# A recurrence's value side: one pair of heads at a time, or two pairs side by side

## The chip, the cores and the metric

The kernel runs on one core of a Trainium2 chip. The metric is the device time of one execution in microseconds. The engines are TensorE (PE, with its weight loads listed as PEld), VectorE (DVE), ScalarE (ACT), GpSimd (POOL) and SyncE (SP), whose queue issues the transfers.

## The reference, cut to what matters

Two decoder layers on 256 tokens of width 2048, in fp32. The first is an RWKV-7 layer with an MLP, the second an attention layer with an MLP. The change lies in the RWKV layer. Its core is a scan over time with a 64x64 state for each of 32 heads, behind it a normalisation over each head, a bonus term, a gate and an output product:

```python
def step(S, inp):
    r_t, w_t, k_t, v_t, a_t, b_t = inp
    sa = jnp.einsum('bhvk,bhk->bhv', S, a_t)
    S = S * w_t[:, :, None, :] + sa[..., None] * b_t[:, :, None, :] + v_t[..., None] * k_t[:, :, None, :]
    y_t = jnp.einsum('bhvk,bhk->bhv', S, r_t)
    return S, y_t
...
y = (y - mu) * lax.rsqrt(var + GN_EPS)
y = y * ln_w.astype(f32).reshape(h, n) + ln_b.astype(f32).reshape(h, n)
y = y + jnp.sum(rh * kh * r_k.astype(f32), axis=-1, keepdims=True) * vh
return (y * g) @ w_out
```

## The kernel before, in words

**Products.** All large products are made of two-part numbers: a weight is split into a high part `wh` (ACT, line 146) and a low part `wl` (DVE, line 147), 512 columns at a time, in `high_low`. Each part comes from a pool of three buffers. `product` makes 128 columns of r or v: sixteen steps, each one wide matmul of 512 columns (line 348) and one of 256 with the low part (line 350); four steps use one split, and each step is reckoned at 0.32.

**The scan.** Time is cut into four chunks of 64 (`NCH`). Heads go in pairs: head 0 on partitions 0 to 63, head 1 on 64 to 127. The key side (`key_low` to `merges`) has made for each pair a triangular inverse `XT` and scaled copies of its inputs and put them to memory (`sp`). The value side then runs the 16 pairs one after the other. `prep_load` brings a pair's data back (`S1b`), `prep` makes the scores `SC` (`sc`, line 908) and the transposes (`bt`, lines 926 to 928), `bonus` the bonus term, and `chain` goes through the chunks: `g` from the scores and the state `SV` (line 966), R times the state into `y` (972), `sa` = `XT` times `G` (976), `sp` the new part of the state (983), the scores times `ST` into `y` (996). DVE carries each result to the next step; POOL makes `Se`, the decayed old state (994), which DVE adds (990). `post` normalises on DVE and POOL; `post_pe` makes the gate with `g2` (line 689), transposes the result (1034), and ACT, POOL and DVE make z from it (1036 to 1041), the input of the output product `wout`.

**What sets the order.** On PE the order is that of the program text (`rwkv_in_order`). Between two dependent steps `chain` calls `hop`, 11 times a pair. A hop first takes what hangs at its number in `extra` (PR: the two parts of the next pair's `prep` at hops 5 and 8; the bonus at 2; `post_pe` of the last pair, loads and splits at hop 2, matmuls at hop 6), subtracts what it is reckoned at from `target`, and `fill`s the rest with steps of the products for later pairs, or at the end of `wout` (`out_part`, lines 681 to 683). The other engines run in an order that the scheduler sets by priority in program order. PSUM has eight banks: two each of `acc`, `ps` and `mg`, one each of `y` and `gn`; `g`, `sa` and `sp` take `mg` in turn, `y` the bank of its name, `post_pe` takes `gn`. The pool `xb` has 16 tiles, at this point for z; `xa` has 32, for the two parts of r's and v's inputs.

Of the kernel before, what the change touches and what calls it, by code (L numbers as in the profile page):

```python
# [17 lines left out]
P = 128  # L18
T = 256
# [76 lines left out]
S1W = 7 * T + 4  # L96


def s1_views(x):
    def c3(a, w=64):  # L100
        return x[:, a:a + NCH * w].rearrange("p (c t) -> p c t", c=NCH)
    bk = x[:, 2 * T:4 * T].rearrange("p (c a t) -> p c a t", c=NCH, a=2)
    return c3(0), c3(T), bk, x[:, 4 * T:5 * T], c3(5 * T, 65), c3(6 * T + 4)


class K:
# [125 lines left out]
    def rstd_row(self, rs, name):  # L232
        nc = self.nc
        ps = self.ps(f"rb_{name}")
        for t in range(2):
            dg = self.sm.tile([P, P], F32, tag="dg", name=f"dg_{name}{t}")
            nc.vector.tensor_scalar(dg, self.c("ident"), rs[:, t:t + 1], None, ALU.mult)
            nc.tensor.matmul(ps[:, t * P:(t + 1) * P], self.ones, dg, start=True, stop=True)
# [29 lines left out]
    def run(self):  # L268
        tc, nc, d = self.tc, self.nc, self.d
        with ExitStack() as es:  # L270
# [6 lines left out]
            self.ones = self.cp.tile([P, P], F32, name="ones")  # L277
# [3 lines left out]
            nc.vector.memset(self.ones, 1.0)  # L281
# [74 lines left out]
    def rwkv(self):  # L356
        tc, nc, d = self.tc, self.nc, self.d
        with ExitStack() as es:
# [3 lines left out]
            self.queue, self.due, self.ob = deque(), 0.0, {}  # L362
            self.side, self.sdue = deque(), 0.0


            self.sp = [dr.tile([2, P, S1W - T], F32, name=f"sp{c}") for c in range(NPAIR // 2)]
            self.za = [dr.tile([64, 32, 64], F32, name=f"za{i}") for i in range(2)]
# [100 lines left out]
            self.hwa = [wk.tile([96, 2, T], F32R, name=f"hwa{i}") for i in range(2)]  # L468
# [55 lines left out]
            merge = chain.from_iterable(self.merges(c, ats) for c in range(8))  # L524
# [46 lines left out]
            ready = set()  # L571

            def products():
                while stream:
                    p, i = stream.popleft()
                    yield from rv_product(p, i)
                    if i == 2:
                        ready.add(p)

# [23 lines left out]
            for p in range(NPAIR):  # L603
                if p in (1, 2):
                    merge_steps(4)
                if p == 13:
                    self.queue.append(take(w0, 28))
                extra = deque([(2, self.bonus(p, rvs[p], st[p]))])
                if p > 0:
                    pe = self.post_pe(p - 1, post, zs)  # L610
                    extra += [(PH - PG, pe), (PH, pe)]
                if p + 1 < NPAIR:
                    st[p + 1] = self.prep_load(p + 1)
                    need(p + 1)
                    pr = self.prep(p + 1, rvs[p + 1], st[p + 1])
# [3 lines left out]
                if p == NPAIR - 1:  # L619
                    extra.insert(1, (2, start(w1)))  # L620
                hop = [0]
                target = (left / (NPAIR - p) + LP) / 11
# [9 lines left out]
                yps = self.chain(p, st.pop(p), hopf)  # L632
                while extra:
                    next(extra.popleft()[1], None)
                post = self.post(p, yps, self.ob[p])
            self.fill(100.0)
            self.drain(self.post_pe(NPAIR - 1, post, zs))
# [127 lines left out]
    def key_mid(self, p, k, side):  # L765
# [12 lines left out]
        for j in J:  # L778
            _, A, BK, kp, E, _ = V[j]
# [4 lines left out]
            nc.sync.dma_start(self.sp[p // 2][j, :, :S1W - 2 * T], S1[j][:, T:S1W - T])  # L784
# [3 lines left out]
    def key_high(self, p, V, ats):  # L788
        nc, wk = self.nc, self.wk
        H = [slice(0, 64), slice(64, 128)]  # L790
        for j in range(2):
            q = p + j
            _, A, BK, _, _, _ = V[j]
# [4 lines left out]
            AT = wk.tile([P, NCH, 64], F32, tag="t1", bufs=10, name=f"AT{q}")  # L798
# [32 lines left out]
    def merges(self, c, ats):  # L831
# [17 lines left out]
        off = two("mk", "mk")[1]  # L849
# [17 lines left out]
        Q, Qv = two("sv", "Q")  # L867
# [9 lines left out]
        Qv = two("sv", "Q32")[1]  # L877
# [6 lines left out]
        nc.sync.dma_start(self.sp[c][:, :, S1W - 2 * T:].rearrange("i p t -> p i t"),  # L884
# [3 lines left out]
    def prep_load(self, p):  # L888
        S1 = self.wk.tile([P, S1W], F32, tag="S1", bufs=2, name=f"S1b_{p}")
        self.nc.sync.dma_start(S1[:, T:], self.sp[p // 2][p % 2])  # L890
        return {"S1": S1}


    def prep(self, p, rv, st):
        nc, wk = self.nc, self.wk
        S1 = st["S1"]
        R, A, BK, kp, E, XT = s1_views(S1)
        RA = S1[:, :2 * T].rearrange("p (a c t) -> p c a t", a=2, c=NCH)
        H = [slice(0, 64), slice(64, 128)]
        r, v = rv[:, :T], rv[:, T:]  # L900
        nc.vector.tensor_tensor(R, self.c4(r), E[:, :, 1:], ALU.mult)

        SC = [[None] * NCH for _ in range(2)]
        msc = self.c("msc")
        pss = [self.ps(f"sc{p}{h}").rearrange("p (c t) -> p c t", c=NCH) for h in range(2)]
        for c in range(NCH):
            for h in range(2):
                nc.tensor.matmul(pss[h][:, c, :], BK[H[h], c].rearrange("p a t -> p (a t)"), RA[H[h], c],
                                 start=True, stop=True)
        for a in (0, 2):  # L910
            for h in range(2):
                x = wk.tile([P, 2, P], F32, tag="t1", bufs=10, name=f"SC{p}{h}{a}")
                nc.vector.tensor_tensor(x, pss[h][:, a:a + 2], msc.unsqueeze(1).broadcast_to([P, 2, P]), ALU.mult)
                nc.gpsimd.tensor_copy(x[H[h], :, 64:], A[H[h], a:a + 2])
                SC[h][a], SC[h][a + 1] = x[:, 0], x[:, 1]
        yield 1.75

        kr = [H[1], H[0]]
        idh = [self.c("ident")[x, x] for x in H]
        ST = self.t2("st", f"ST{p}").rearrange("p (c h t) -> p c h t", c=NCH, h=2)  # L920
        SV = self.t2("sv", f"SV{p}").rearrange("p (c h t) -> p c h t", c=NCH, h=2)
        BT = self.t2("bt", f"BT{p}").rearrange("p (h c t) -> p h c t", c=NCH, h=2)
        pss = [self.ps(f"bt{p}{h}").rearrange("p (c t) -> p c t", t=64) for h in range(2)]
        for c in range(NCH):
            for h in range(2):
                nc.tensor.transpose(pss[h][:, c, :], BK[H[h], c].rearrange("p a t -> p (a t)"), idh[h])
            nc.tensor.transpose(pss[0][:, 4 + c, :], rv[H[0], T - 64 + 64 * c:T + 64 + 64 * c], idh[0])
            nc.tensor.transpose(pss[1][:64, 4 + c, :], v[H[1], 64 * c:64 * c + 64], idh[1])
        for h in range(2):
            nc.scalar.activation(ST[kr[h], :, h, :], pss[h][kr[h], 4:8, :], AF.Copy)  # L930
            nc.scalar.activation(BT[:, h], pss[h][:, :4, :], AF.Copy)
            nc.gpsimd.tensor_copy(SV[kr[h], :, h, :], ST[kr[h], :, h, :])
        st.update(R=R, E=E, XT=XT, SC=SC, ST=ST, SV=SV, BT=BT)
        yield 0.9

    def bonus(self, p, rv, st):
        nc = self.nc
        r, v = rv[:, :T], rv[:, T:]
        ob = self.t2("ei", f"ob{p}")
        self.ob[p] = ob  # L940
        bv = ob[:, T:]
        nc.vector.scalar_tensor_tensor(bv, r, self.vec("r_k", p), s1_views(st["S1"])[3], ALU.mult, ALU.mult)
        bps = self.ps(f"bon{p}")
        bh = self.wk.tile([P, 2, T], F32R, tag="nr", bufs=WB["nr"], name=f"bh{p}")
        nc.gpsimd.tensor_copy(bh[:, 0], bv)
        nc.vector.tensor_tensor(bh[:, 1], bv, bh[:, 0].bitcast(F32), ALU.subtract)
        for i in range(2):
            nc.tensor.matmul(bps[:, :T], self.bones, bh[:, i], start=(i == 0), stop=(i == 1))
        nc.vector.tensor_tensor(bv, bps[:, :T], v, ALU.mult)
        yield 0.43  # L950


    def chain(self, p, st, hop):
# [3 lines left out]
        R, E, XT, SC, ST, SV, BT = (st[n] for n in ("R", "E", "XT", "SC", "ST", "SV", "BT"))  # L957
        yps = self.ps(f"y{p}", "y")
        for c in range(NCH):
            first = c == 0  # L960
            g = self.ps(f"g{p}{c}", "mg")
            for h in range(2):
                if first:
                    nc.tensor.matmul(g[H[h], :64], SC[h][c][kr[h], 64:], SV[kr[h], c, h, :], start=True, stop=True)
                else:
                    nc.tensor.matmul(g[H[h], :64], SC[h][c][:, 64:], SV[:, c, h, :], start=True, stop=True)
            G = wk.tile([P, 64], F32, tag="G", bufs=2, name=f"G{p}{c}")
            nc.vector.tensor_copy(G, g[:, :64])
            ys = [yps[H[h], c * 64:(c + 1) * 64] for h in range(2)]
            if not first:  # L970
# [312 lines left out]
```

## Time and profile before

| | us |
|---|---|
| median of 3 runs | 2420.58 (2420.09 to 2421.37) |
| the profiled execution | 2418.55 |
| its span | 2416.4 |
| PE busy | 2337.0 (97%) |
| DVE busy | 1558.5 (64%) |
| ACT busy | 1283.8 (53%) |
| POOL busy | 483.0 (20%) |

The span runs from the first to the last instruction of the program; 2.15 us of the execution lie around it. Busy time is the union of an engine's instructions. Matmuls are pipelined and their ends are modelled, so PE's cost is better read from one instruction's start to the next one's start. The key side takes the first 300 us, the value side about 310 to 683 us; the rest is MLP, attention and MLP.

### The profile page before, as it was taken

Reading aid. Unit: us, or ns where it says so; the run is one execution under the profiler, and the core shown is the slowest. Engines: PE = TensorE matmul, PEld = TensorE weight load, DVE = VectorE, ACT = ScalarE, POOL = GpSimd, SP = SyncE. Lnnn points to the kernel's source line nnn. Section 1 sums busy time; section 2 is a strip of 40 time slices with the busy share of each in tenths; the row PEclk is TensorE's granted clock in tenths of the full one; section 3 lists DMA queues with packets and bytes.
Section 4 is the critical chain, followed back from the end, with each engine's and each line's share of the span. In section 5 each row is a group of like instructions: output and inputs, shape, how many; then the busy total and the mean of one; then the engine's idle time right before and its main releaser. Section 6 shows DMA issues by size and latency. Waiting matters only on the chain. (4 is left out here: it accounts for less than half of the span.)

```text
span 2416.4 us, 40472 instructions
## 1 busy us (share of the span) xinstructions
PE 2337.0 (97%) x14448; PEld 1925.1 (80%) x14448; DVE 1558.5 (64%) x3126; ACT 1283.8 (53%) x2563; POOL 483.0 (20%) x635
## 2 busy tenths in 40 slices
PE   5887899999999999999999999999999999999999
PEld 4676677777788888888888887777888888888887
DVE  7887667777666556556556666765655655655655
ACT  5545333333356546546546565665654554654654
POOL 3657322333201101001001001641110110110100
PEclk9999899999999999999999999999999999999999
DMA  4666544444465555555555555334555555555565
GB/s 140 203 197 180 165 144 147 142 142 140 147 198 183 191 189 192 187 195 188 192 192 188 189 185 178 114 114 153 187 187 195 189 189 193 191 189 195 186 199 174
DMA packets 149642, 425.64 MB, mean 176 GB/s; under 512 B 38848, under 2 KB 46784, under 8 KB 149440
## 3 DMA queue, kind: packets, MB, share of 16 engines
q1 hardware_dynamic: 148000, 420.62, 53.1%
q8 instruction: 113, 1.85, 0.3%
q10 hardware_dynamic: 1440, 2.44, 0.3%
q14 instruction: 89, 0.73, 0.1%
HBM read 403.05 MB, written 19.96 MB: 175 GB/s over the span
## 5 line engine op out<-in xcount | busy, mean ns | idle before, releaser
L169 PE MATMUL ps_u<-x_m,wh_u 128*128 128x512 f32 x2048 | 559.1, 394 | 0.0
L147 DVE TENSOR_TENSOR wl_d<-raw_d,wh_d 128x512 fp32r<-128x512 f32 x512 | 355.7, 695 | 293.6 <-ACT wh_d L146 274.4
L147 DVE TENSOR_TENSOR wl_u<-raw_u,wh_u 128x512 fp32r<-128x512 f32 x512 | 354.5, 693 | 263.4 <-ACT wh_u L146 253.7
L146 ACT ACTIVATE wh_d<-raw_d 128x512 fp32r<-128x512 f32 x512 | 323.6, 632 | 351.9 <-DVE wl_d L147 261.3
L146 ACT ACTIVATE wh_u<-raw_u 128x512 fp32r<-128x512 f32 x512 | 323.7, 633 | 246.2 <-PE ps_u L169 227.7
L187 PE MATMUL ps_d<-wl_d,h 128*128 128x512 f32 x1024 | 399.0, 390 | 1.2 <-DVE wl_d L147 1.2
L185 PE MATMUL ps_d<-wh_d,h 128*128 128x512 f32 x1024 | 398.7, 389 | 0.0
L186 PE MATMUL ps_d<-wh_d,h 128*128 128x512 f32 x1024 | 398.6, 389 | 0.0
L169 PEld LDWEIGHTS ps_u<-x_m,wh_u 128*128 128x128 f32 x2048 | 350.6, 189 | 47.6 <-ACT wh_u L146 0.2
L173 PEld LDWEIGHTS ps_u<-x_m,wl_u 128*128 128x128 f32 x2048 | 313.8, 189 | 43.1
L1065 POOL TENSOR_TENSOR h<-w,h 128x256 fp32r<-128x256 f32 x128 | 114.0, 892 | 1117.6 <-ACT h L1064 1079.1
L173 PE MATMUL ps_u<-x_m,wl_u 128*128 128x256 f32 x2048 | 325.7, 281 | 0.0
L187 PEld LDWEIGHTS ps_d<-wl_d,h 128*128 128x128 f32 x1024 | 192.2, 188 | 41.5 <-DVE wl_d L147 1.6
L185 PEld LDWEIGHTS ps_d<-wh_d,h 128*128 128x128 f32 x1024 | 192.2, 188 | 39.8
L186 PEld LDWEIGHTS ps_d<-wh_d,h 128*128 128x128 f32 x1024 | 192.2, 188 | 39.4
L348 PE MATMUL ps_k<-lk,wh_k 128*128 128x512 f32 x256 | 98.1, 420 | 7.0 <-DVE lk L417 6.3
L348 PE MATMUL ps_v<-lv,wh_v 128*128 128x512 f32 x256 | 103.5, 432 | 0.0
L348 PE MATMUL ps_r<-lr,wh_r 128*128 128x512 f32 x256 | 102.9, 431 | 0.0
L146 ACT ACTIVATE wh_v<-raw_v 128x512 fp32r<-128x512 f32 x64 | 40.4, 631 | 94.7 <-PE ps_r L348 36.2
L146 ACT ACTIVATE wh_r<-raw_r 128x512 fp32r<-128x512 f32 x64 | 40.3, 630 | 79.8 <-PE ps_v L348 32.9
L350 PE MATMUL ps_k<-lk,wl_k 128*128 128x256 f32 x256 | 74.9, 292 | 6.3 <-DVE wl_k L147 6.3
L1222 POOL TENSOR_SCALAR s<-s,den 128x128 f32<-128x128 f32 x64 | 61.8, 981 | 77.3 <-DVE den L1218 30.5
(308 smaller groups left out, 3747.3 us busy)
## 6 DMA issues: line engine op xcount, KB each, us to landing
raw_u<-in_up SPq DMA_DIRECT2D x256, 512.0 KB
raw_d<-in_down SPq DMA_DIRECT2D x256, 512.0 KB
raw_k<-in_wrkv SPq DMA_DIRECT2D x32, 512.0 KB
raw_r<-in_wrkv SPq DMA_DIRECT2D x32, 512.0 KB
raw_v<-in_wrkv SPq DMA_DIRECT2D x32, 512.0 KB
raw_wout<-in_wout SPq DMA_DIRECT2D x32, 512.0 KB
raw_q<-in_wq SPq DMA_DIRECT2D x32, 512.0 KB
S1b<-sp SPq DMA_DIRECT2D x16, 770.0 KB
```

The source lines that it names most:

```text
L146: nc.scalar.activation(wh, src, AF.Copy)
L147: nc.vector.tensor_tensor(wl, src, wh.bitcast(F32), ALU.subtract)
L169: nc.tensor.matmul(ps, wh[:, j * P:(j + 1) * P], xt[kt].rearrange("p a t -> p (a t)"), start=(kt == 0), stop=False, skip_group_check=True)
L173: nc.tensor.matmul(ps[:, :T], wl[:, j * P:(j + 1) * P], xt[kt][:, 0, :], start=False, stop=(kt == KT - 1), skip_group_check=True)
L185: nc.tensor.matmul(pss[t], xt[kb][:, 0, tt], wh, start=(kb == 0), stop=False)
L186: nc.tensor.matmul(pss[t], xt[kb][:, 1, tt], wh, start=False, stop=False)
L187: nc.tensor.matmul(pss[t], xt[kb][:, 0, tt], wl, start=False, stop=(kb == nk - 1))
L348: nc.tensor.matmul(ps, wh[:, j * P:(j + 1) * P], xt[kt].rearrange("p a t -> p (a t)"), start=(kt == 0), stop=False, skip_group_check=True)
L350: nc.tensor.matmul(ps[:, :T], wl[:, j * P:(j + 1) * P], xt[kt][:, 0, :], start=False, stop=(kt == KT - 1), skip_group_check=True)
L1065: nc.gpsimd.tensor_tensor(hx[:, 1, :], w, hx[:, 0, :].bitcast(F32), ALU.subtract)
L1222: nc.gpsimd.tensor_scalar(ss[i][:, sl[t]], ss[i][:, sl[t]], den[:, i, t:t + 1], None, ALU.mult)
```

## The change

Two pairs (a duo) go through `chain` together, so that the loop runs 8 times. Each step is issued for both pairs, into one bank; the carrying copies of the second pair go to ACT instead of DVE. R times the state stands behind `sa` instead of behind `g`. The decayed old state is no longer made on POOL and added on DVE: PE adds the old state to `sp` with a matmul by the identity (chunks 1 and 2), and the decay is applied once when the sum is carried out. Four of the second pair's tiles (RX, ST, SV, BT) come from `xb`; `XT` is put to memory by itself (`sx`) and loaded beside a copy of R, so `S1b` is shorter. `prep` makes the bonus too and hangs in six parts at hops 5 to 10, and asks for its pair's products (`need`) there. `post_pe` takes two g2 tiles at hop 2, makes both pairs at hop 4 and takes both banks of `mg`; its result waits in `zf` until all products are made (`self.made`), and `split_z` makes z from it, for the first half in `xa`. The merges of 6 and 7 move from between the first pairs into hops 1 to 4 of duo 0. `wout` is queued at hop 10 of duo 6 and hop 2 of duo 7. `rstd_row` makes its matrix of ones when it is called. Lines that leave stand in the functions above; of `post` only the loop over two pairs is new.

```diff
...
-PH, PR = 6, (5, 8)
-PG = 4
+PG, PH, PR = 2, 4, (5, 6, 7, 8, 9, 10)
 PB = dict(acc=2, ps=2, mg=2, y=1, gn=1)
-WB = dict(rv=3, bt=2, st=2, sv=2, ta=2, sq=2, ei=2, nr=2, mk=1)
+WB = dict(rv=3, bt=2, st=2, sv=2, ta=2, sq=2, ei=2, nr=2, mk=1, rx=2, hb=2)
...
+            ND = NPAIR // 2
+            for u in range(ND):
+                extra = deque()
+                if u == 0:
+                    late = [self.merges(c, ats) for c in (6, 7)]
+                    extra += [(k, m) for k in (1, 2, 3, 4) for m in late]
+                if u > 0:
+                    pe = self.post_pe(u - 1, post, zs)
+                    extra += [(PG, pe), (PH, pe)]
+                if u + 1 < ND:
+                    st[u + 1] = self.prep_load(u + 1)
+                    pr = self.prep(u + 1, rvs, st[u + 1], need)
                     extra += [(k, pr) for k in PR]
+                if u == ND - 2:
+                    extra.append((PR[-1], start(w0)))
+                if u == ND - 1:
+                    extra.append((2, start(w1)))
                 left = len(stream) * 5.1 + LW
                 extra = deque(sorted(extra, key=lambda e: e[0]))
                 hop = [0]
+                target = (left / (ND - u) + LP) / 11
                 def hopf():
...
+    def duo(self, tag, j, name):
+        return self.xlt(name, F32, "xb") if j else self.t2(tag, name)
+    def prep_load(self, u):
+        res = []
+        for j in range(2):
+            S1 = self.wk.tile([P, S1W], F32, tag="S1", bufs=2, name=f"S1b_{2 * u + j}")
+            self.nc.sync.dma_start(S1[:, T:], self.sp[u][j])
+            RX = self.duo("rx", j, f"RX{2 * u + j}")
+            self.nc.sync.dma_start(RX[:, T:], self.sx[u][j])
+            res.append({"S1": S1, "RX": RX})
...
+    def prep(self, u, rvs, sts, need=None):
...
+        for j in range(2):
+            p, st = 2 * u + j, sts[j]
+            if need:
+                need(p)
...
+            nc.vector.tensor_tensor(R, self.c4(r), E[:, :, 1:], ALU.mult)
+            st["R"], st["XT"] = self.c4(st["RX"][:, :T]), self.c4(st["RX"][:, T:])
+            nc.gpsimd.tensor_copy(st["R"], R)
+            st["eC"] = self.sm.tile([P, NCH], F32, tag="eC", bufs=4, name=f"eC{p}")
+            nc.gpsimd.tensor_copy(st["eC"], E[:, :, 64])
+            st["bv"] = bv
...
+            yield 1.3
...
+            ST = self.duo("st", j, f"ST{p}").rearrange("p (c h t) -> p c h t", c=NCH, h=2)
+            SV = self.duo("sv", j, f"SV{p}").rearrange("p (c h t) -> p c h t", c=NCH, h=2)
+            BT = self.duo("bt", j, f"BT{p}").rearrange("p (h c t) -> p h c t", c=NCH, h=2)
...
+            st.update(ST=ST, SV=SV, BT=BT)
...
+            yield 0.8
...
+            yield 0.25
...
+    def chain(self, u, sts, hop):
...
+        yps = [self.ps(f"y{2 * u + j}", ("y", "gn")[j]) for j in J]
+        def bank(nm, c):
+            return self.ps(f"{nm}{u}{c}", "mg")[:, :P].rearrange("p (j t) -> p j t", j=2)
         for c in range(NCH):
+            first, last = c == 0, c == NCH - 1
+            g = bank("g", c)
+            for j in J:
+                for h in range(2):
+                    x = kr[h] if first else full
+                    nc.tensor.matmul(g[H[h], j], SC[j][h][c][x, 64:], SV[j][x, c, h, :], start=True, stop=True)
+            G = wk.tile([P, 2, 64], F32, tag="G", bufs=2, name=f"G{u}{c}")
+            nc.vector.tensor_copy(G, g)
+            hop()
+            sap = bank("sa", c)
+            for j in J:
+                for h in range(2):
+                    nc.tensor.matmul(sap[H[h], j], XT[j][H[h], c, :], G[H[h], j], start=True, stop=True)
             for h in range(2):
+                nc.vector.tensor_copy(ST[0][H[h], c, h, :], sap[H[h], 0])
+                nc.scalar.activation(ST[1][H[h], c, h, :], sap[H[h], 1], AF.Copy)
+            ys = [[yps[j][H[h], c * 64:(c + 1) * 64] for h in range(2)] for j in J]
             if not first:
+                for j in J:
+                    for h in range(2):
+                        nc.tensor.matmul(ys[j][h], R[j][H[h], c, :], SV[j][H[h], c, h, :], start=True, stop=False)
+            hop()
+            if not last:
+                sp = bank("sp", c)
+                for j in J:
+                    if not first:
+                        for h in range(2):
+                            nc.tensor.matmul(sp[H[h], j], ident[:, H[h]], SV[j][:, c, h, :], start=True, stop=False)
+                    for h in range(2):
+                        nc.tensor.matmul(sp[H[h], j], BT[j][:, h, c, :], ST[j][:, c, h, :], start=first, stop=True)
                 for h in range(2):
+                    nc.vector.tensor_scalar(SV[0][H[h], c + 1, h, :], sp[H[h], 0], eC[0][H[h], c:c + 1], None, ALU.mult)
+                    nc.scalar.activation(SV[1][H[h], c + 1, h, :], sp[H[h], 1], AF.Copy, scale=eC[1][H[h], c:c + 1])
+            for j in J:
                 for h in range(2):
+                    nc.tensor.matmul(ys[j][h], SC[j][h][c][:, :64], ST[j][:, c, h, :], start=first, stop=True)
+            if not last:
                 hop()
         return yps
...
+    def post_pe(self, u, post, zs):
+        nc = self.nc
+        lg = []
+        for j in range(2):
+            raw = self.load(self.d["g2"][2 * u + j].rearrange("p a c -> p (a c)"), f"g2_{2 * u + j}")[0][:, :2 * P]
+            lg.append(self.high_low(raw, f"g2_{2 * u + j}"))
         yield 0.0
         H = [slice(0, 64), slice(64, 128)]
+        zf = self.xlt(f"zf{u}", F32, "xb").rearrange("p (j t) -> p j t", j=2)
+        pss = [self.ps(f"yt{2 * u + j}", "mg") for j in range(2)]
         for j in range(2):
+            for i in range(2):
+                self.three(pss[j][:, T:], [x[:, i * P:i * P + P] for x in lg[j]], [x[:, i] for x in self.sg], i == 0, i == 1)
+        for j in range(2):
+            p, (yc, bv) = 2 * u + j, post[j]
+            yt, gp = pss[j][:, :T], pss[j][:, T:]
+            for c in range(NCH):
+                for h in range(2):
+                    nc.tensor.matmul(yt[H[h], c * 64:(c + 1) * 64], yc[H[h], c, :], self.c("ident")[H[h], H[h]],
+                                     start=True, stop=True)
+            o = self.t2("ei", f"o{p}")[:, :T]
+            nc.scalar.activation(o, yt, AF.Identity, bias=self.vec("ln_b", p), scale=self.vec("ln_w", p))
+            nc.gpsimd.tensor_tensor(o, o, bv, ALU.add)
+            nc.vector.tensor_tensor(zf[:, j], gp, o, ALU.mult)
+        self.zf.append((u, zf))
+        if self.made:
+            self.split_z(zs)
+        yield 3.4
+    def split_z(self, zs):
+        nc = self.nc
+        while self.zf:
+            u, zf = self.zf.popleft()
+            for j in range(2):
+                zt = self.xlt(f"z_{2 * u + j}", F32R, ("xa", "xb")[u >= NPAIR // 4])
+                nc.scalar.activation(zt[:, 0, :], zf[:, j], AF.Copy)
+                nc.vector.tensor_tensor(zt[:, 1, :], zf[:, j], zt[:, 0, :].bitcast(F32), ALU.subtract)
+                zs.append(zt)
```

## Rows read from the trace of the kernel before

**Rows 1.** The page: engines over the whole span, and the granted clock in 40 slices.
```profile
PE 2337.0 (97%) x14448; PEld 1925.1 (80%) x14448; DVE 1558.5 (64%) x3126; ACT 1283.8 (53%) x2563; POOL 483.0 (20%) x635
...
PEclk9999899999999999999999999999999999999999
```

**Rows 2.** Table by stage: busy us (instructions) of PE, PEld, DVE, ACT, POOL; clock, DMA.
```profile
310.00:672.00 362.00, 358.80 (x3376) 273.62 (x3374) 262.05 (x722) 137.30 (x283) 120.56 (x220) 1.00 0.43 143
1000.00:1200.00 200.00, 200.00 (x1000) 169.71 (x999) 117.35 (x187) 107.63 (x194) 13.96 (x16) 1.00 0.58 192
```

**Rows 3.** Waits of PE in the value stage: us in total, times, longest us.
```profile
PE g L966 <- DVE SV L990: 2.3, 7, 0.6
```

**Rows 4.** Timeline of PE, two stretches: start us, us, engine, line, operation, tiles, shapes, count.
```profile
443.35 0.34 PE L983 MATMUL sp<-ST,BT 128*64 128x64 f32 x4
443.51 0.29 PE L996 MATMUL y<-ST,SC 128*64 128x64 f32 x4
443.73 0.50 PE L689 MATMUL yt<-sg,wh_g 128*128 128x256 f32 x2
...
450.32 0.40 PE L348 MATMUL ps_v<-lv,wh_v 128*128 128x512 f32 x1
450.56 0.28 PE L350 MATMUL ps_v<-lv,wl_v 128*128 128x256 f32 x1
450.67 0.40 PE L348 MATMUL ps_v<-lv,wh_v 128*128 128x512 f32 x1
450.91 0.28 PE L350 MATMUL ps_v<-lv,wl_v 128*128 128x256 f32 x1
451.12 0.34 PE L966 MATMUL g<-SV,SC 128*64 128x64 f32 x4
451.39 0.33 PE L972 MATMUL y<-SV,S1b 64*64 64x64 f32 x4
451.65 0.50 PE L348 MATMUL ps_r<-lr,wh_r 128*128 128x512 f32 x1
451.99 0.28 PE L350 MATMUL ps_r<-lr,wl_r 128*128 128x256 f32 x1
```

**Rows 5.** Timeline of a pair's `post_pe` and of the chain step behind it.
```profile
444.63 0.68 PE L1034 MATMUL yt<-cst,y 64*64 64x64 f32 x16
...
445.42 0.56 ACT L1036 ACTIVATE ob<-yt,par 128x256 f32<-128x256 f32 x1 [0.17 <-PE yt L1034]
...
445.59 0.65 PE L966 MATMUL g<-SV,SC 128*64 128x64 f32 x4 [0.27 <-DVE SV L990]
...
445.90 1.52 POOL L994 TENSOR_SCALAR Se<-SV,S1b 64x64 f32<-64x64 f32 x2
...
447.51 0.74 POOL L1037 TENSOR_TENSOR ob<-ob 128x256 f32<-128x256 f32 x1
...
449.64 0.42 DVE L1038 TENSOR_TENSOR ob<-yt,ob 128x256 f32<-128x256 f32 x1
```

**Rows 6.** Timeline of the last `post_pe`, at the end of the stage.
```profile
671.51 0.68 PE L1034 MATMUL yt<-cst,y 64*64 64x64 f32 x16
...
673.71 0.42 DVE L1038 TENSOR_TENSOR ob<-yt,ob 128x256 f32<-128x256 f32 x1 [0.86 <-POOL ob L1037]
```

**Rows 7.** Waits of ACT in the value stage: us in total, times, longest us.
```profile
ACT wh_r L146 <- PE ps_v L348: 30.0, 19, 2.7
...
ACT wh_r L146 <- PE yt L689: 16.1, 7, 3.1
```

**Rows 8.** Timeline: the two halves of one split.
```profile
439.85 0.63 ACT L146 ACTIVATE wh_v<-raw_v 128x512 fp32r<-128x512 f32 x1 [1.08 <-PE ps_v L348]
...
440.76 0.68 DVE L147 TENSOR_TENSOR wl_v<-raw_v,wh_v 128x512 fp32r<-128x512 f32 x1
```

**Rows 9.** Table of two stretches of the stage before; the clock is the third last column.
```profile
271.00:274.30 3.30, 2.22 (x87) 1.85 (x83) 2.42 (x5) 1.38 (x3) 0.00 (x0) 1.00 0.81 238
274.30:277.70 3.40, 3.40 (x11) 2.61 (x10) 0.35 (x2) 1.00 (x2) 0.00 (x0) 0.50 0.95 328
```

More of the change, by code (lines that the diff above doesn't have):

```diff
@@ L92 @@
 CST2, CAT2 = _consts2()
-S1W = 7 * T + 4
+S1W = 6 * T + 4
 def s1_views(x):
@@ L234, in rstd_row @@
         ps = self.ps(f"rb_{name}")
+        ones = self.sm.tile([P, P], F32, tag="ones", name=f"ones_{name}")
+        nc.vector.memset(ones, 1.0)
         for t in range(2):
@@ L237, in rstd_row @@
             nc.vector.tensor_scalar(dg, self.c("ident"), rs[:, t:t + 1], None, ALU.mult)
-            nc.tensor.matmul(ps[:, t * P:(t + 1) * P], self.ones, dg, start=True, stop=True)
+            nc.tensor.matmul(ps[:, t * P:(t + 1) * P], ones, dg, start=True, stop=True)
         rb = self.sm.tile([P, T], F32, tag="rb", name=f"rbs_{name}")
@@ L361, in rwkv @@
             self.wk = wk
-            self.queue, self.due, self.ob = deque(), 0.0, {}
+            self.queue, self.due = deque(), 0.0
             self.side, self.sdue = deque(), 0.0
             self.sp = [dr.tile([2, P, S1W - T], F32, name=f"sp{c}") for c in range(NPAIR // 2)]
+            self.sx = [dr.tile([2, P, T], F32, name=f"sx{c}") for c in range(NPAIR // 2)]
             self.za = [dr.tile([64, 32, 64], F32, name=f"za{i}") for i in range(2)]
@@ L467, in rwkv @@
             lora_out = {}
-            self.hwa = [wk.tile([96, 2, T], F32R, name=f"hwa{i}") for i in range(2)]
+            self.hwa = [wk.tile([P, 2, T], F32R, tag="hb", bufs=2, name=f"hwa{i}")[:96] for i in range(2)]
             lw_, la_ = (lora1(3, "w1", 96, "w1", "ps", lerp_pool, ("st", "bt")),
@@ L523, in rwkv @@
             ats = {}
-            merge = chain.from_iterable(self.merges(c, ats) for c in range(8))
+            merge = chain.from_iterable(self.merges(c, ats) for c in range(6))
             def step(i):
@@ L631, in hopf @@
                         self.fill(t)
[L632 removed]
+                yps = self.chain(u, st[u], hopf)
                 while extra:
                     next(extra.popleft()[1], None)
[L635 removed]
+                post = self.post(u, yps, st.pop(u)[0]["bv"])
             self.fill(100.0)
[L637 removed]
+            self.drain(self.post_pe(ND - 1, post, zs))
             for _ in range(2):
@@ L848, in merges @@
                     nc.sync.dma_start(x[0][H[h]], z[h, :, :, 256 * i0:256 * i0 + 512])
-        off = two("mk", "mk")[1]
+        off = two(("mk", "hb")[c == 7], "mk")[1]
         at = [ats[2 * c + i] for i in range(2)]
@@ L866, in merges @@
         X = X[1]
-        Q, Qv = two("sv", "Q")
+        tq = ("sv", "ei")[c == 7]
+        Q, Qv = two(tq, "Q")
         nc.scalar.activation(Qv, mm("p16_", H, H, each(off), full, X, full), AF.Copy)
@@ L876, in merges @@
         ps = mm("p32_", hi, lo, at, B, X, A)
-        Qv = two("sv", "Q32")[1]
+        Qv = two(tq, "Q32")[1]
         for h in range(2):
@@ L894, in prep @@
[L894 to L950, printed above, removed]
@@ L953, in chain @@
-    def chain(self, p, st, hop):
+    def duo(self, tag, j, name):
[8 more added lines that the diff above has]
+            res.append({"S1": S1, "RX": RX})
+        return res
@@ L1020, in post_pe @@
-    def post_pe(self, p, post, zs):
+        res = []
+        for j in range(2):
+            p = 2 * u + j
+            y3 = self.c4(yps[j][:, :T])
+            mu = wk.tile([P, NCH], F32, tag="mu", bufs=2, name=f"mu{p}")
+            nc.vector.tensor_reduce(mu, y3, AX.X, ALU.add)
+            nc.vector.tensor_scalar(mu, mu, 1.0 / 64, None, ALU.mult)
+            ya = self.t2("ta", f"y{p}").rearrange("p (a c t) -> p a c t", a=2, c=NCH)
+            yc, ysq = ya[:, 0], ya[:, 1]
+            nc.vector.tensor_tensor(yc, y3, mu.unsqueeze(2).broadcast_to([P, NCH, 64]), ALU.subtract)
+            nc.gpsimd.tensor_tensor(ysq, yc, yc, ALU.mult)
+            var = wk.tile([P, NCH], F32, tag="var", bufs=2, name=f"var{p}")
+            nc.vector.tensor_reduce(var, ysq, AX.X, ALU.add)
+            nc.vector.tensor_scalar(var, var, 1.0 / 64, GN_EPS, ALU.mult, ALU.add)
+            ry = self.rsqrt(var, NCH, f"gn{p}")
+            nc.vector.tensor_tensor(yc, yc, ry.unsqueeze(2).broadcast_to([P, NCH, 64]), ALU.mult)
+            res.append((yc, bv[:, j]))
@@ L1028, in post_pe @@
-        ps = self.ps(f"yt{p}", "gn")
-        yt, gp = ps[:, :T], ps[:, T:]
+        zf = self.xlt(f"zf{u}", F32, "xb").rearrange("p (j t) -> p j t", j=2)
+        pss = [self.ps(f"yt{2 * u + j}", "mg") for j in range(2)]
         for j in range(2):
-            self.three(gp, [x[:, j * P:j * P + P] for x in lg], [x[:, j] for x in self.sg], j == 0, j == 1)
-        for c in range(NCH):
-            for h in range(2):
-                nc.tensor.matmul(yt[H[h], c * 64:(c + 1) * 64], yc[H[h], c, :], self.c("ident")[H[h], H[h]],
-                                 start=True, stop=True)
@@ L1036, in post_pe @@
-        nc.scalar.activation(o, yt, AF.Identity, bias=self.vec("ln_b", p), scale=self.vec("ln_w", p))
-        nc.gpsimd.tensor_tensor(o, o, bv, ALU.add)
-        nc.vector.tensor_tensor(o, gp, o, ALU.mult)
-        zt = self.xlt(f"z_{p}", F32R, "xb")
-        nc.scalar.activation(zt[:, 0, :], o, AF.Copy)
-        nc.vector.tensor_tensor(zt[:, 1, :], o, zt[:, 0, :].bitcast(F32), ALU.subtract)
-        zs.append(zt)
-        yield 1.8
+            for i in range(2):
+                self.three(pss[j][:, T:], [x[:, i * P:i * P + P] for x in lg[j]], [x[:, i] for x in self.sg], i == 0, i == 1)
@@ new lines, in post_pe @@
+        for j in range(2):
+            p, (yc, bv) = 2 * u + j, post[j]
+            yt, gp = pss[j][:, :T], pss[j][:, T:]
+            for c in range(NCH):
+                for h in range(2):
+                    nc.tensor.matmul(yt[H[h], c * 64:(c + 1) * 64], yc[H[h], c, :], self.c("ident")[H[h], H[h]],
+                                     start=True, stop=True)
+            o = self.t2("ei", f"o{p}")[:, :T]
+            nc.scalar.activation(o, yt, AF.Identity, bias=self.vec("ln_b", p), scale=self.vec("ln_w", p))
+            nc.gpsimd.tensor_tensor(o, o, bv, ALU.add)
+            nc.vector.tensor_tensor(zf[:, j], gp, o, ALU.mult)
```

141 lines of the change are left out of this document (56 added, 85 removed).

## The prediction

> **What bounds the kernel now.** I read the page first: TensorE (PE) is busy for 97% of the span, and its granted clock dips in one slice only, from 240 to 300 us [rows 1]. The table by stage comes next. In the value stage, 310 to 672 us, where every line of the change lies, PE is busy for 358.8 of 362 us at full clock, VectorE (DVE) for 262, ScalarE (ACT) for 137 and GpSimd (POOL) for 121. In the MLP behind it PE is busy for 200 of 200 us [rows 2]. So time that PE gains or loses in the value stage passes through to the end. The list of waits says that PE hardly stands still there: its longest entry is 2.3 us [rows 3]. A busy PE is not a PE at its peak, though, and the instructions one by one show what the busy share hides [rows 4]. Inside a product a wide matmul and its low part take 0.35 us from start to start (450.32 to 450.67), the low part 0.11 of it. Around the narrow matmuls of the chain four extra pieces appear: the last low part before them takes 0.21 instead of 0.11 (450.91 to 451.12), the first wide one behind them 0.34 instead of 0.24 (451.65 to 451.99), and four narrow instructions take 0.16 with a slow beginning alone (443.35 to 443.51), 0.22 with a slow end alone (443.51 to 443.73) and 0.27 with both (451.12 to 451.39). So four cost 0.12 bare, the beginning 0.05 and the end 0.10. One excursion from wide to narrow and back costs 0.09 + 0.05 + 0.10 + 0.09 = 0.33 us besides its work, and a change between two kinds of narrow work 0.15.
>
> **Part by part.** *Two pairs side by side.* `chain` calls `hop` 11 times; that stays, but it is called for 8 duos instead of 16 pairs. I followed the generators step by step and counted the places where PE goes from narrow to wide work: 180 before from the first merge on, 108 after; 72 fewer at 0.33 us are 23.8 us. Changes between kinds of narrow work: 125 before, 34 after (R·SV stands behind `sa` of the same 64x64 shape instead of behind the 128x64 `g`; `sc` and `bt` meet fewer chain steps), 91 at 0.15 us are 13.6 us. Together -37.4 us.
>
> Is the price one of the shape, or of the wait in front of each group? From `g` to R·SV nothing new is waited for, and the step still takes 0.27 us; from `sp` to the last `y`, both 128x64, it is 0.16 [rows 4]. The Trainium skill says it so: changing the tiling mode, not just the tile, drains the engine (TensorEngine Tiling (Array Packing), Key Properties). By that rule R·SV beside `sa` is free, which the rows support; were it the wait, those 48 changes would stay and the sum would be 7 us worse.
>
> *The state's sum on PE* adds a matmul with the identity for each head in chunks 1 and 2: 16 pairs x 2 chunks, four narrow instructions each, at 0.12 us: +3.8 us. It replaces `Se` on POOL, which is off PE's path (one pair of them took 1.52 us, [rows 5]).
>
> *A stall that goes.* Today `post_pe` lies at hop 6 with no product behind it, and `g` follows its transposes at once: 16 of them start at 444.63 and `g` at 445.59 [rows 5]. 16 narrow ones with both edges are 0.63 us, so 0.33 of these 0.96 us is waiting for the state, and as much again inside `g` (busy 0.65 instead of 0.34). In the new order that wait has other work in front. Over 15 pairs that is at most 10 us, at least the 2.3 us that the waits list; I take -8, near the upper row.
>
> *Two splits of g2 held at once.* `post_pe` now splits two g2 tiles at hop 2 and uses them at hop 4. The pools `wh` and `wl` still have three buffers. In the old kernel one was held, two were left for the products, and PE did not wait [rows 3]; but ACT did: its splits wait for a product's buffer, and several times until g2's matmuls (L689) gave theirs back [rows 7]. With two held, one is left: the next 512 columns can be split only when PE has finished the last ones. A split took 1.59 us from the start of ACT's half to the end of DVE's (439.85 to 440.76 + 0.68, [rows 8]); with about 0.15 of hand-overs, and less the 0.35 that PE would have spent until the next low part anyway, PE stands 1.39 us at each. By `target` a hop is filled with 2.1 falling to 1.7 now, at 0.32 a step: hops 2 and 3 hold 10 to 13 product steps, four to a split (in duo 7 six steps of `wout`, two to a split), by the generators 20 boundaries in the seven duos that have a `post_pe` in their loop. Three of them fall on a chain step, which hides about 0.8 us each: 20 x 1.39 - 2.4 = +25 us. Below: 0.63 + 0.68 with no queue on DVE, 20 x 1.1 - 2.4 = 20, and 0 if product splits go ahead of g2's. Above: behind one more DVE operation of 0.69 at half the boundaries, 32.
>
> *Both banks of `mg` for `post_pe`.* `yt` of both pairs now sits in `mg`, and `g`, `sa` and `sp` live in the same two banks. `sa` of chunk 1, next in PE's order and with no product in between (3.4 is charged against a hop of about 2), must wait until the first `yt` is read: ACT, POOL and DVE in turn. At the quiet end of the stage that took 1.94 us from the last transpose (671.51 + 0.68 to 673.71 + 0.42, [rows 6]); in the middle 4.75 us (445.31 to 450.06, [rows 5]), of which most was POOL busy with `Se` and DVE with other work. The second pair's transposes cover 0.5. `Se` is gone and PE's own stop empties DVE's queue, so I stay near the low end: 1.7 us, seven times, +12 us (10 to 30).
>
> *Small ones.* At the very end z of both last pairs is late: the two steps with z14 used to cover z15's way through the engines. Now PE has nothing until z14 is there: 1.94 + 0.4 for its split - 0.5 of transposes plus the low half, about +2.5. In duo 0 the merges of 6 and 7 run in `mg` at hops 1 to 4 without products between them, each waiting for the last one's evacuation of about 0.6 us: +4 (0 to 8). In duo 6 the products are used up at hop 8, `wout` starts at hop 10, and twelve z splits come at once: +3 (0 to 6). The clock: in the stage before, PE busy for 2.22 of 3.30 us was followed by a stretch at half clock, 1.2 GHz [rows 9]. At hops 2 to 4 PE will pause in a like manner; a half-clock stretch of 3.4 us [rows 9] costs some 1.5 us of wide work, and I put two of them in, +3 (0 to 12).
>
> *At nothing.* ACT gets 112 narrow copies. Even at the 0.56 us of a 128x256 one [rows 5] that is 63 us on an engine that is idle for 225 of 362 us, and each has a hop of products to hide in; without the cover each would cost PE that long. DVE gets less to do. `S1b` moves the same bytes in two transfers, and a duo's load is issued five hops ahead; SP's queue also carries the weights, at 192 GB/s in the MLP [rows 2], so there is room. `ones`, `hb` and the z tiles in `xa` move nothing on PE.
>
> **The sum.** -37.4 + 3.8 - 8 + 25 + 12 + 2.5 + 4 + 3 + 3 = +7.9 us. The profiled execution took 2418.55 us (span 2416.4), so 2426.5; the median of the runs is 2.0 higher, which gives 2428.5. I predict 2428 us. A measurement of this kernel tells 0.2%, about 4.8 us, from no change.
>
> **Rivals.** *Product splits are not held up* (0.20): the splits of the next products go ahead of g2's, or g2's come late. For it: the order on ACT is a scheduler's, not written out. Against it: [rows 7] show splits standing until L689. Without the +25 and with less loss of clock: 2418.55 - 19 + 2 = about 2402, faster. *Neither new wait shows* (0.07): also without the +12, about 2390; against it, two banks are two banks. *The half clock sets in at every `post_pe`* (0.12): the one-buffer stretch and the stop at `sa` together starve PE, each duo loses one half-clock stretch (1.5 us) and the bank wait is 3.5 us instead of 1.7: 7 x (1.5 + 1.8) - 3 more than assumed, about 2448, slower. It decides if the clock falls in these stretches at all, as it did after the one of [rows 9]; the value stage so far shows none [rows 2]. *The switch price stays* (0.06): if the edges come with each dependent group and not with each excursion, only half of 37.4 is saved: about 2447.
>
> **How the numbers follow.** My forecast has 0.55. Its own range from the bounds above is 2412 to 2444; about a sixth of it lies below 2416 and a quarter within 0.2% of the old time. The 8-in-10 range reaches to the first rival: 2402 to 2448. Faster: 0.09 + 0.19 + 0.07 = 0.35. Same: 0.14 + 0.01 = 0.15. Slower: 0.32 + 0.12 + 0.06 = 0.50.
>
> **What would show it.** Switches: the stretches of wide work in the value stage number about 100 where they were 171. Buffers: PE gets waits for `wl` (DVE L147's line) or `wh` in hops 2 and 3 of each duo, about 20 in all near 1.4 us; today there is none. Banks: `sa` waits for the DVE operation that writes `zf`, seven times 1.5 us or more. The end: about 2 us of idle PE behind the last transposes. I am wrong if the waits of PE in the value stage add up to less than 25 us, or if the stage without its waits is not about 40 us shorter.

## The result and the profile after

The changed kernel takes 2441.04 us (median; 2436.74 to 2442.85) beside 2420.34 for the one before on the same chip: ratio 1.0085, 95% interval 1.0068 to 1.0103. It is slower. The profiled execution took 2442.85 us, its span 2441.0.

Page of the changed kernel, as [rows 1]:

```profile
PE 2330.6 (95%) x14576; PEld 1931.3 (79%) x14576; DVE 1530.7 (63%) x2983; ACT 1313.0 (54%) x2675; POOL 455.8 (19%) x603
...
PEclk8988889999999999999999999999999999999999
```

PE is busy 6 us less in a span 25 us longer. The clock digit is 8, below 0.90, in five slices where it was in one. Four of them lie in the first 305 us, where the clock of both kernels moves between 0.86 and 1.00 by stretches of 60 us; new is the dip from 300 to 360 us, 0.80 against 1.00. Table by stretch of the changed kernel, columns as in [rows 2]: the value stage, its worst part, its steady part, a piece at the end.

```profile
308.00:694.00 386.00, 347.20 (x3544) 274.65 (x3542) 234.86 (x585) 167.45 (x397) 90.53 (x187) 0.97 0.43 136
...
334.20:351.20 17.00, 15.96 (x258) 13.49 (x258) 5.61 (x14) 4.94 (x13) 0.40 (x1) 0.50 0.18 64
...
378.00:640.00 262.00, 234.08 (x2379) 184.69 (x2379) 167.98 (x430) 117.42 (x285) 67.91 (x142) 1.00 0.42 134
...
696.00:699.40 3.40, 3.38 (x8) 2.70 (x9) 0.97 (x2) 0.72 (x2) 0.00 (x0) 0.50 0.25 101
```

PE pauses for 39 of 386 us, where it paused for 3 of 362. The steady part is at full clock, so its 28 us of pauses are waits; the 17 us from 334.2 are at 1.2 GHz with PE nearly always busy, on merges above all. The waits of PE in the value stage of the changed kernel (columns as [rows 3]) name them:

```profile
PE sa L999 <- DVE zf L1074: 10.6, 7, 1.5
PE ps_r L348 <- ACT wh_r L146: 5.2, 8, 0.7
PE ps_v L348 <- ACT wh_v L146: 4.8, 8, 0.7
PE bt L952 <- DVE SC L940: 3.8, 4, 1.9
PE ps_v L350 <- DVE wl_v L147: 2.7, 8, 0.7
PE ps_r L350 <- DVE wl_r L147: 2.1, 9, 0.3
PE x L866 <- DMA XT<-zx: 2.1, 2, 1.1
PE ps_wo L686 <- ACT z L1087: 2.0, 1, 2.0
```

The first line is the wait for both banks, seven times. The two `wh` and the two `wl` lines are the splits that come too late, 16 or 17 of each, 14.8 us in all. One split in the timeline of the changed kernel:

```profile
425.90 0.28 PE L350 MATMUL ps_v<-lv,wl_v 128*128 128x256 f32 x1
...
426.16 0.63 ACT L146 ACTIVATE wh_v<-raw_v 128x512 fp32r<-128x512 f32 x1 [0.33 <-PE ps_v L348]
...
426.82 0.69 DVE L147 TENSOR_TENSOR wl_v<-raw_v,wh_v 128x512 fp32r<-128x512 f32 x1
...
426.84 0.49 PE L348 MATMUL ps_v<-lv,wh_v 128*128 128x512 f32 x1 [0.66 <-ACT wh_v L146]
...
427.57 0.38 PE L350 MATMUL ps_v<-lv,wl_v 128*128 128x256 f32 x1 [0.23 <-DVE wl_v L147]
...
427.79 0.40 PE L348 MATMUL ps_v<-lv,wh_v 128*128 128x512 f32 x1
```

ACT begins only when PE has released the one free buffer. PE's steps start 0.94 apart instead of 0.11 before the high part (+0.82, by unrounded starts) and 0.73 instead of 0.24 before the low one (+0.49): 1.31 us a split. The wait for the banks, same timeline:

```profile
436.99 1.15 PE L1069 MATMUL yt<-cst,y 64*64 64x64 f32 x32
...
437.77 1.03 ACT L1072 ACTIVATE o<-yt,par 128x256 f32<-128x256 f32 x2 [0.17 <-PE yt L1069]
...
438.42 1.40 POOL L1073 TENSOR_TENSOR o<-o,bv 128x256 f32<-128x256 f32 x2 [9.63 <-ACT o L1072]
...
439.17 0.42 DVE L1074 TENSOR_TENSOR zf<-yt,o 128x256 f32<-128x256 f32 x1 [0.84 <-POOL o L1073]
...
439.65 0.45 PE L999 MATMUL sa<-G,RX 64*64 64x64 f32 x8 [1.52 <-DVE zf L1074]
439.93 0.40 PE L1007 MATMUL y<-SV,RX 64*64 64x64 f32 x8
```

`sa` stands until ACT, POOL and DVE have read the first `yt`. `sa` and R·SV, 16 instructions of one shape, follow without a slow end: 0.28 from one group to the next.

The account below is worked out from PE's start times. "Edges" are the changes of shape at the prices of [rows 4]; "rest" is the elapsed time less the work at full price and less the edges, so it holds the waits and the half clock. Two pairs of before stand beside one duo.

| stretch | before: elapsed, edges, rest (us) | after: elapsed, edges, rest (us) |
|---|---|---|
| first preparation | 5.8, 0.7, 1.5 | 18.9, 1.3, 7.5 |
| duo 0 | 63.6, 11.5, 0.9 | 51.9, 4.9, 11.7 |
| duos 1 to 5 | 201.2, 44.6, 6.9 | 217.6, 23.0, 31.3 |
| duo 6 | 39.8, 9.0, 1.5 | 44.0, 4.4, 9.1 |
| duo 7 | 57.1, 9.2, 0.6 | 53.2, 4.1, 3.8 |
| tail, to the MLP | 52.9, 2.2, -1.3 | 56.6, 2.3, 2.1 |
| sum | edges 77, rest 10.0 | edges 40, rest 65.6 |

Work moves between stretches (440 product steps in both kernels), so edges and rest are what to compare: edges -37, rest +55.6, the work itself +3.5. The stage ahead, whose products and merges the change leaves alone, was 3.1 us longer in this execution. That is scatter: with the same stage ahead the first `sc` starts at 307.77 us here, and between 302.5 and 305.8 in the seven further runs below that have it; it was 304.70 before. Together the MLP starts at 750.07 instead of 725.08 us (+25.0) and lasts the same.

### The profile page after: what moved, and what is told of

Read it like the earlier page. It is cut to its first block, busy times and chain, and to the rows that moved or that the text cites. A ratio compares the mean times of both kernels' runs of the same rounds, so it can differ in the third digit from the quotient of the medians.

```text
span 2441.0 us, 40716 instructions
## 1 busy us (share of the span) xinstructions
PE 2330.6 (95%) x14576; PEld 1931.3 (79%) x14576; DVE 1530.7 (63%) x2983; ACT 1313.0 (54%) x2675; POOL 455.8 (19%) x603
## 5 line engine op out<-in xcount | busy, mean ns | idle before, releaser
L186 PEld LDWEIGHTS ps_d<-wh_d,h 128*128 128x128 f32 x1024 | 192.2, 188 | 39.8
L350 PE MATMUL ps_r<-lr,wl_r 128*128 128x256 f32 x256 | 74.7, 292 | 2.1 <-DVE wl_r L147 2.1
L350 PE MATMUL ps_v<-lv,wl_v 128*128 128x256 f32 x256 | 74.0, 289 | 2.7 <-DVE wl_v L147 2.7
```

What stands on the lines that cost most here:

```text
L186: nc.tensor.matmul(pss[t], xt[kb][:, 1, tt], wh, start=False, stop=False)
L350: nc.tensor.matmul(ps[:, :T], wl[:, j * P:(j + 1) * P], xt[kt][:, 0, :], start=False, stop=(kt == KT - 1), skip_group_check=True)
```

## The experiments

Each run was timed beside the kernel before; ratios are to that.

**One split for both g2 tiles** (e1, the change otherwise):

```diff
+raw = self.wraw.tile([P, 1024], F32, tag="raw", ...)[:, :4 * P]
 for j in range(2):
-    raw = self.load(self.d["g2"][2 * u + j]...)[0][:, :2 * P]
-    lg.append(self.high_low(raw, f"g2_{2 * u + j}"))
+    nc.sync.dma_start(raw[:, 2 * P * j:2 * P * (j + 1)], self.d["g2"][2 * u + j]...)
+both = self.high_low(raw, f"g2_{u}")
```

> The changed kernel, but both g2 tiles of a duo are loaded into one tile and split once, 512 columns, so that one buffer of wh and of wl is held from hop 2 to hop 4 and not two. Theory (one buffer is left for the products, and PE waits at every split boundary in hops 2 and 3): the 20 stands of about 1.3 us in seven duos go, 25 us less: 2416 us, and the trace shows no wait of L348 or L350 for wh or wl inside the duos, while sa still waits 7 times 1.7 us for zf. Rival (ACT and DVE are late with the splits because the chain's copies moved to ACT and the merged steps crowd them): the waits stay for the most part, one operation less on each engine is worth 2 to 4 us: 2438 us.

2418.25 us, 1.0001 (0.9993 to 1.0010): 0.84% less than the change, some 20 us. The list of waits of PE in e1 begins:

```profile
PE sa L999 <- DVE zf L1075: 10.6, 7, 1.5
PE sc L935 <- DVE bv L970: 3.9, 1, 3.9
PE bt L952 <- DVE SC L940: 3.7, 4, 1.8
```

The four split lines are gone and the bank wait is untouched; the rest of duos 1 to 7 falls from 44.2 to 25.3 us. The held buffer costs 19 to 20 us.

**No charge behind `post_pe`** (e2): products may go between its transposes and `sa`.

```diff
-        yield 3.4
+        yield 0.0
```

> The changed kernel, but post_pe is reckoned at 0 and not 3.4, so that hop 4 is filled with product steps (2.1 by the target) between the second pair's transposes and sa. Theory (sa stands 1.7 us because both banks of mg are taken and nothing lies in front of it): the products cover the wait, 12 us less: 2429 us, and the seven waits of sa for zf are gone. Rival (the reading of both yt is slow in itself, and products behind post_pe only move the wait, since DVE and ACT then make splits first): sa still waits 1 us or more each time: 2436 to 2441 us.

2433.22 us, 1.0064 (1.0052 to 1.0077), 0.2% or 5 us less than the change; less than expected. The `sa` wait is gone from the list, the split waits stay, as here in e2:

```profile
PE ps_v L348 <- ACT wh_v L146: 4.8, 8, 0.7
PE ps_r L348 <- ACT wh_r L146: 4.6, 7, 0.7
```

The products let in make one more excursion in a duo, so edges rise by 2 us where rest falls by 8.

**All merges before the stage** (e3): 6 and 7 as well, and none in duo 0.

```diff
-merge = chain.from_iterable(self.merges(c, ats) for c in range(6))
+merge = chain.from_iterable(self.merges(c, ats) for c in range(8))
...
-            merge_steps(M0 - 8)
+            merge_steps(M0)
```

> The changed kernel, but the merges of 6 and 7 run before the first prep with a product fill of 1.4 behind each of their eight steps, as the other merges do, and not in hops 1 to 4 of duo 0. Theory (without products between them they starve PE, which then runs 17 us at half clock in duo 0): the half clock behind 330 us goes and with it 10 us, the waits inside the merges another 5, eight excursions of 0.33 us come back: 2428 us. Rival (the half clock comes from the start of the value side, the first prep, whatever the merges do): the same stretch shows, 2438 to 2444 us.

2448.69 us, 1.0127 (1.0113 to 1.0140): slower, the wrong sign. Waits of PE in e3, 270 to 400 us:

```profile
PE p L865 <- DMA X<-zx: 11.6, 2, 6.5
PE bt L951 <- DVE SC L939: 3.7, 1, 3.7
```

The merges now stand for their own data and part of that stretch is at half clock, but duo 0 has no half clock left and its rest is 1.3 us instead of 11.7. So duo 0's loss hangs on the merges; moved earlier it only moves: the stage ahead takes 29.9 us more for 19 us more work, and duos 1 to 5 have 5.7 us more rest. **All three together** (e4) took 2418.77 us, 1.0001 (0.9992 to 1.0011), 28 us above the theory's number: by e7 below, which leaves the merges where they are, moving them cost 4 us and did not give 13, and splits and banks give 24 to 27 us and not 37.

> The changed kernel with all three: one g2 split, products behind post_pe, merges before the first prep. Theory: the three losses are separate and add up, 25 + 12 + 13 = 50 us less than the changed kernel: 2391 us, 29 us below the kernel before; what is left against the saved edges are the identity matmuls and the wait for z at the end. Rival (the saving in edges is not worth what I reckon, and the freed time is lost elsewhere, at DVE or at the transfers): not below 2410 us.

**e1 and e2 together** (e7), the base of the next three:

> One split for both g2 tiles and no charge behind post_pe, nothing else. If the two costs are separate (theory): 2441 - 22.8 - 7.8 = 2410 us, with no split wait and no wait of sa for zf. If the two stands overlap or one grows when the other goes (rival): nearer 2418.

2415.15 us, 0.9985 (0.9975 to 0.9994). By the ratios -1.0% against the change; e1 and e2 alone add up to -1.04%. The costs are separate, in the rest as well (27 us, and 19 and 8 alone); the 2410 subtracted medians that stood beside different runs of the kernel before. From 378 to 565 us, table as in [rows 2]:

```profile
378.00:565.00 187.00, 182.79 (x1879) 148.69 (x1879) 127.89 (x325) 88.78 (x210) 59.04 (x112) 1.00 0.47 151
```

PE pauses for 4 of 187 us. Rest of duos 1 to 7: 17.1 us.

**Products between duo 0's merges** (e8):

```diff
-late = [self.merges(c, ats) for c in (6, 7)]
+late = [(0.0 for _ in self.merges(c, ats)) for c in (6, 7)]
```

> As e7, and the merges in hops 1 to 4 of duo 0 are reckoned as 0, so that products go between them. Theory: the half clock of 17 us there comes from giving PE merges alone; it goes, and duo 0 loses some 5 us less: 2405. Rival: the merges wait for their own copies and the clock follows from the first preparation's stands before; the half clock stays and the time is that of e7.

2411.88 us, 0.9969 (0.9960 to 0.9979). Duo 0's rest falls from 13.1 to 7.7 and its half clock from 9.9 to 3.4 us: the theory's 5 us; the rival is out. (e7's 13.1 is the highest of the five runs with this start, the lowest is 10.2.) By the medians 3.3 us are left of it: half is lost again in duo 6 (7.6 to 10.2, half clock 3.2 to 10.2), in a profiled execution that was the slowest of the nine.

**More products in the first preparation** (e9): `self.fill(1.0)` becomes `self.fill(2.5)` there.

> As e7, and the first preparation is filled with 2.5 instead of 1.0 between its steps. Theory: its 7 to 9 us of loss are waits for copies that the filler doesn't meet, so it keeps them and the time stays that of e7, within 2 us. Rival: they are lack of wide work; 5 us less.

2409.78 us, 0.9965 (0.9955 to 0.9975). The preparation keeps its loss (7.1 us), as expected, with another wait on top of the list of e9:

```profile
PE ps_v L350 <- DVE wl_v L147: 5.3, 2, 5.2
```

But duo 0 loses 4.5 us less, with 3.4 us of half clock instead of 9.9, which was not expected: its merges are as bare as in e7. Wide work ahead of them (47 product steps instead of 19) also kept the clock up. The time is the rival's, 5 us less, the place is not.

**The end** (e10): what is left of `wout` goes behind the last transposes, and `wout` begins at hop 8 of duo 6.

```diff
-            self.fill(100.0)
+            self.fill(5.0)
             self.drain(self.post_pe(ND - 1, post, zs))
+            self.fill(100.0)
...
-extra.append((PR[-1], start(w0)))
+extra.append((PR[3], start(w0)))
```

> As e7, and at the end only: wout begins at hop 8 of duo 6 instead of hop 10, and what is left of it goes behind the last post_pe's transposes. Theory: duo 6 loses 4 us less and the tail's wait of 2 us and its half-clock stretch go, 3.8 us less: 2402. Rival: wout's splits at hop 8 meet those of z and of the last products, and duo 6 gains nothing: 2406.

2410.47 us, 0.9964 (0.9950 to 0.9977). The tail's 3.4 us go, wait and half clock both; duo 6 loses 1.9 us less, half of what was expected.

**e7 to e10 in one** (e5, which ran before them):

> The changed kernel with the one g2 split and the products behind post_pe, and four edits where its trace shows the rest of the loss: the merges stay in hops 1 to 4 of duo 0 but are reckoned at 0, so that each of these hops is filled with products; the first prep gets a fill of 2.5 behind each of its six parts and not 1.0; wout is queued at hop 8 of duo 6 and not at hop 10; the last fill stops after 5 us, so that some of wout is left to cover z14. Theory (the rest of the loss is PE without wide work, at the first prep 7 us, in duo 0 11, in duo 6 9, at the end 3): the first two edits of the former runs leave about 2410 us, and these four take 20 to 25 off: 2388 us, with under 7 us at half clock between 300 and 420 us where there were 23. Rival (these stretches are bound by DVE and ACT or by the merges' own chain of evacuations, and products in front of them only add to the time): not below 2405 us.

2402.76 us, 0.9939 (0.9925 to 0.9953): faster than both kernels, though some 15 us short of what was expected. Table of e5 for the change's worst part and the steady part:

```profile
334.00:351.00 17.00, 14.05 (x289) 11.91 (x291) 8.72 (x20) 6.45 (x15) 1.04 (x2) 1.00 0.24 80
...
378.00:565.00 187.00, 183.67 (x1928) 149.57 (x1928) 128.64 (x334) 90.55 (x216) 62.22 (x119) 1.00 0.49 153
```

The clock is full where it was half. What it keeps: 7.5 us in the first preparation, 6.8 in duo 0, 5.8 in duo 6.

**The kernel before, with R·SV behind `sa`** (e6): same work, same waits, only the order of shapes.

```diff
-            if not first:
-                for h in range(2):
-                    nc.tensor.matmul(ys[h], R[...], SV[...], ...)
             hop()
             ...  # sa
+            if not first:
+                for h in range(2):
+                    nc.tensor.matmul(ys[h], R[...], SV[...], ...)
```

> The kernel before with one edit: R times the state is issued behind sa and not behind g, so that 64x64 matmuls stand beside 64x64 ones. Nothing else differs, neither the work nor the waits nor the hops. Theory (a change of the tile shape costs about 0.15 us, whatever is waited for): 48 such changes go, 7 us less than before, 2412 us, and the trace has no group of R times the state that follows g. Rival (the price belongs to each dependent group, and the shape has no part in it): 2418 to 2420 us, as before.

2410.47 us, 0.9962 (0.9950 to 0.9974). Timeline of PE in e6:

```profile
444.93 0.33 PE L973 MATMUL sa<-G,S1b 64*64 64x64 f32 x4
445.09 0.28 PE L976 MATMUL y<-SV,S1b 64*64 64x64 f32 x4
...
448.13 0.34 PE L966 MATMUL g<-SV,SC 128*64 128x64 f32 x4
448.39 0.50 PE L348 MATMUL ps_r<-lr,wh_r 128*128 128x512 f32 x1
```

`sa` to R·SV takes 0.16 us with one shape on both sides; [rows 4] have 0.27 behind `g`. The price belongs to the change of shape, not to each dependent group.

## Why the prediction came out as it did

The forecast (2428) had the sign; the time was 13 us over it, near the upper end of the forecast's own range (2412 to 2444). In the two profiles, +25.0 where the sum had +7.9, term by term:

- **Edges, -37.4, and the identity, +3.8: right.** -37 and +3.5. Excursions in the stage fell from 171 to 99, as counted. The rival in which the price stays is refuted by e6, and by `g`: eight instructions take 0.38 us to the next start where four took 0.27 ([rows 4]), so that a group pays its edges once. The Trainium skill's rule in TensorEngine Tiling (Array Packing), Key Properties, that a change of tiling mode drains the engine and a change of tile doesn't, agrees with e6's 0.16 against 0.27 us.

```profile
435.00 0.45 PE L992 MATMUL g<-SV,SC 128*64 128x64 f32 x8
435.38 0.51 PE L694 MATMUL yt<-sg,wh_g 128*128 128x256 f32 x2
```

- **"A stall that goes", -8: right, somewhat large.** Two pairs in the timeline of the kernel before, the one of [rows 5] and one that does not wait:

```profile
445.59 0.65 PE L966 MATMUL g<-SV,SC 128*64 128x64 f32 x4 [0.27 <-DVE SV L990]
446.17 0.33 PE L972 MATMUL y<-SV,S1b 64*64 64x64 f32 x4
...
650.23 0.68 PE L1034 MATMUL yt<-cst,y 64*64 64x64 f32 x16
650.84 0.34 PE L966 MATMUL g<-SV,SC 128*64 128x64 f32 x4
651.10 0.33 PE L972 MATMUL y<-SV,S1b 64*64 64x64 f32 x4
```

  Without a wait `g` starts 0.61 us behind the first transpose and takes 0.26 to the next start; in [rows 5] it is 0.96 and 0.58. Over the 15 pairs the excess is 2.9 us in front of `g` and 3.6 inside it: 6.5 us, of the 10.0 that are the whole stage's rest. In the changed kernel `g` waits once in the list, 0.8 us, and not behind `post_pe`.
- **Split stands, +25: right in kind, a little large.** There are 16, where 20 were counted, of 1.31 us each against 1.39: 21 us. e1 takes out 19 to 20 us. The rival in which the products' splits are not held up is out.
- **Both banks, +12: right as a stand, less as a price.** Seven times 1.71 us from start to start (1.52 behind the transposes' modelled end) are 11.9, but removing it (e2) frees 8 us of rest, 6 after the new edges. Taken out together (e7), splits and banks are 27 us, not the 33 that they stood. Short waits come in their place; those for ACT's copies, put at nothing, are not in the change's list. In e7, 375 to 565 us:

```profile
PE g L992 <- ACT SV L1020: 1.6, 5, 0.5
PE sp L1017 <- ACT ST L1002: 1.5, 3, 0.7
```

- **Duo 0 and the clock, +4 and +3, and the first preparation at no price: the step that failed.** First preparation and duo 0 lost 16.8 us more than before. I put the half clock where PE would wait in hops 2 to 4 of the later duos; it fell nowhere there (1.00 from 378 to 640). It fell where PE was given narrow work with little wide between: 6.8 us around the preparation and 17.1 in duo 0. In the 7.2 us ahead of the latter, PE was busy for 4.63:

```profile
327.00:334.20 7.20, 4.63 (x143) 4.10 (x142) 2.72 (x8) 1.63 (x4) 1.29 (x4) 1.00 0.66 221
```

  The first preparation had no term at all: it now makes two pairs and their bonus in six parts, with 19 product steps for cover, where it made one pair in two parts. It lost 7.5 us instead of 1.5. Together +16.8 where the sum had +7. The rival with a half clock at every `post_pe` named the mechanism in the wrong place.
- **Duo 6, +3, and the tail, +2.5.** With splits and banks out of the way (e7) duo 6 still has 6.1 us more rest than before; the tail has 3.4, of which the z wait is 2.0 as said and a half-clock stretch the remainder.

In sum: the rest of duos 1 to 7 in the changed kernel is 44.2 us, 21.3 of split stands, 11.9 of bank stands and 11.0 of others; before it was 9.0, 6.3 of the stall and 2.7 of others. So the others grew by 8.3 us where the sum had 3 (duo 6): +5. With the start of the stage (+10), the stage ahead (+3), the stall (+2) and the tail (+1), less 4 for the splits, that is 17 us. By the measured median the surplus is 13. That the forecast came this close owes something to luck: 4 us too much in one place stand against 21 too little in others.

Of the two signs of being wrong the first did not show: the listed waits of PE add up to 40 us. The second can't be read off busy time (347.2 us against 358.8, 12 less), which holds the half clock and parts of the stands. By the account the stage without its rest is 376.7 us instead of 410.4, 34 shorter.

Open: how much of the first preparation's 7 us its longest stand costs. The trace of the changed kernel has DVE idle there for 6.2 us behind POOL, whose `bh`, a part of the bonus that is now in `prep`, waits for a store:

```profile
318.07 0.40 POOL L964 CAST bh<-bv 128x256 fp32r<-128x256 f32 x1 [9.49 <-DMA sx<-XT]
...
318.51 0.48 DVE L965 TENSOR_TENSOR bh<-bv,bh 128x256 fp32r<-128x256 f32 x1 [6.24 <-POOL bh L964]
```

The store takes the `XT` of the last merge in front to memory; it was issued at 310.43 us. `bh` and this `XT` are both of the pool `nr`, which has two tiles. DVE stands there for 6.2 to 6.8 us in all eight runs that keep the last merges in duo 0, whatever wait leads PE's list. In e3 and e4 it is 2.0 and 1.6 us, and the preparation loses its 7 us all the same, there with DVE waiting 2.8 and 3.2 us for a load of `S1b`. No run took the stand away.

Open too: whether in duo 0 the half clock is the cause of the loss or goes with the same lack of work. In the five runs with this start it lies between 9.9 and 17.1 us and the rest between 10 and 13, and they do not go together (e10 had 13.5 us of half clock and a rest of 10.4, e7 9.9 and 13.1).

## What to carry to other kernels

Before interleaving two chains, count what each shared pool must hold at the new depth: the saving here (37 us of shape changes) was real and was given back by one staging buffer (20 us), one bank wait and a start without filler. Price the start of the loop as well as its steady part: the first preparation had no term, and it and duo 0 cost 17 us. Grouping small matmuls by shape is worth doing alone (e6: one block moved, 0.4%).

## What was not expected of the hardware

A PE that is busy for 15.96 of 17.0 us ran all of them at half clock, on 258 mostly small matmuls. Wide work ahead of that stretch raised the clock as well as wide work inside it: duo 0 has 9.9 to 17.1 us of half clock in the five runs that leave its start as it is, and 3.4 in e9 and in e8.
